# The mixers' own transfers and the residual's load issued by GpSimd's queue instead of SyncE's

## The chip, the cores and the metric

The kernel runs on one core of a Trainium2 chip. The metric is the device time of one execution in microseconds (us). The engines are named as in the profile: PE is TensorE (the matrix engine), DVE is VectorE, ACT is ScalarE, POOL is GpSimd and SP is SyncE, which here does nothing but issue transfers (DMAs). Each engine works through its own instructions in a fixed order; between engines there are only semaphores.

## The reference

One layer of a hybrid decoder over 256 tokens of width 2048, all in float32. Four mixers, each 512 wide, read parts of one projection, and their results go through a common output projection; then comes a SwiGLU of 5632 hidden columns and a final norm.

```python
n = rmsnorm(x, attn_norm[l])
u = n @ w_in[l]
u_gdn, u_mlstm, u_rglru, u_rwkv = jnp.split(u, MIXER_SPLITS, axis=-1)
y_gdn = gated_deltanet(u_gdn, ...)
y_mlstm = mlstm(u_mlstm, ...)
y_rglru = rglru_block(u_rglru, ...)
y_rwkv = rwkv7_time_mix(u_rwkv, ...)
mix = jnp.concatenate([y.astype(x.dtype) for y in (y_gdn, y_mlstm, y_rglru, y_rwkv)], axis=-1)
x = x + mix @ w_out[l]
n = rmsnorm(x, ffn_norm[l])
x = x + (jax.nn.silu(n @ ffn_w_gate[l]) * (n @ ffn_w_up[l])) @ ffn_w_down[l]
return rmsnorm(x, final_norm)
```

gated_deltanet and rwkv7_time_mix work in chunks of 64 tokens, and each needs the inverse of a triangular block per chunk and head. mlstm needs running sums and running maxima of its gates over the tokens.

## The kernel before

**Weights.** All weights lie in device memory as 404 units of 128x1024 float32 (512 KB). `raw()` loads a unit from SP's queue into one of four raw buffers; `halves()` makes two halves of it, whi on ACT (a copy rounded to the format that PE multiplies) and wlo on DVE (the rest), into four buffers each; `mm3()` multiplies with three matmuls (whi·hi, whi·lo, wlo·hi). In the profile the loads and the halves stand under L274, the matmuls under L169, L170 and L171, with the tiles big, mx and mxl as their results in PSUM.

**Mixers.** Each mixer is a Python generator: rw (rwkv7_time_mix, `rwkv_half`, one for each half of the heads), gd (gated_deltanet, `gdn_half`), ml (mlstm) and rg. While the big projections are written out, `tick` advances the generators, and their own small matmuls go through `Lag` (recorded as L409 and L413), so that the scheduler puts them between the big ones. The scheduler settles the order on every engine when the kernel is built.

**The transfers that the change touches**, all issued by SP before:

- rw: each half writes its triangular blocks to device memory (L622, eight pieces of 32x8x32) and loads them into the solver's tile (L625). `joint_solve` inverts all blocks together on DVE (L499, L500) and writes the inverse (L512) and, after a copy on DVE (L503), its transpose (L513) back to device memory, 64x1024 each. Each half loads its part of both into a tile XT (L660, L661: twelve transfers of 32x8x32 in all; sD_321 and sD_325 in the order's names). The first products that use them are the zu matmuls, `mx<-sD,sD 32x32`.
- gd: the same with L932, L933, L512, L513 (32x1024 here), L945 and L946 (fourteen transfers of 32x4x32). Its first products are copied by DVE in L955 and L963.
- ml: the gate weights (L782, L784), the running sums ncd (L822), the running maxima Md (L848), and for each half a broadcast of two rows of them over 128 partitions (`bcast_rows`, L866). L1059 and L1060 on DVE read Md's broadcast.
- `w_out`: four loads of the residual x, 512 KB each (L1196).

POOL before clears tiles, takes a few powers, issues one load for rg (L1419, 512 KB) and, late in the program, four broadcasts of the final norm's weights (L1301, 256 KB each). L763 on DVE is the mixers' convolution.

Of the kernel before, what the change touches and what calls it, by code (L numbers as in the profile page):

```python
# [12 lines left out]
P = 128  # L13
T = 256
# [491 lines left out]
def joint_solve(em, key, q0, nq, steps, free=False):  # L506
    nc = em.nc
    while not all((key + "A", h) in em.mix for h in range(2)):
        yield
    yield from solve_blocks(em, q0, nq, steps)  # L510
    dt, dtt = (em.dp.tile([nq, 32, 32], F32, name=em.nm("dr"), tag=em.nm("dr")) for _ in range(2))
    nc.sync.dma_start(dt, em.inv[q0 : q0 + nq])  # L512
    nc.sync.dma_start(dtt, em.blk[q0 : q0 + nq])  # L513
    em.mix[key + "S"] = (dt, dtt)
    if free:
        em.free(*em.solver)


def rwkv_half(em, hf, LX, R, K, V):
    nc = em.nc  # L520
# [12 lines left out]
    z = lora(em.lw[0:64], LX[0:64, 0:T])  # L533
# [3 lines left out]
    z = lora(em.lw[64:128], LX[64:128, 0:T])  # L537
    a = em.S()
# [4 lines left out]
    z = lora(em.g2, LX[:, T : 2 * T])  # L543
# [23 lines left out]
    z = yield from sums(em, em.bdr, sq, 1)  # L567
# [28 lines left out]
    z = yield from sums(em, em.bdr, t1, 1)  # L596
# [6 lines left out]
    for cc in range(2):  # L603
        zz = [em.mx(), em.mx()]
        g = em.S(2)
        gv = g.rearrange("p (c j h n) -> p c j h n", c=2, j=2, h=2)
        for h in range(2):
            rows = slice(64 * h, 64 * h + 64)
            for ci in range(2):
                for j in range(2):  # L610
                    u = j * 4 + 2 * cc + ci
                    ts = slice(u * 64, u * 64 + 64)
                    o = (ci * 2 + j) * P
                    em.pe.matmul(zz[h][:, o : o + P], KB[rows, u * P : u * P + P], ARv[rows, :, ts], start=True, stop=True)
        for h in range(2):
            nc.vector.tensor_tensor(g.rearrange("p (u h n) -> p u h n", h=2, n=P)[:, :, h, :], zz[h].rearrange("p (u n) -> p u n", n=P), em.gm.unsqueeze(1).to_broadcast([P, 4, P]), op=ALU.mult)
        GM.append(g)
        dr = em.dp.tile([32, 32, 32], F32, name=em.nm("dr"), tag=em.nm("dr")) if cc == 0 else dr
        for d in range(2):
            q0 = cc * 16 + d * 8  # L620
            src = g[64 + 32 * d : 96 + 32 * d, :].rearrange("p (u n) -> p u n", n=P)[:, :, 32 * d : 32 * d + 32]
            nc.sync.dma_start(dr[q0 : q0 + 8].rearrange("q s t -> s q t"), src)  # L622
        yield

    nc.sync.dma_start(blk3, dr)  # L625

    def gmv(c, h, s):
        return GM[c // 2][:, (c % 2) * 512 + h * P + s * 64 : (c % 2) * 512 + h * P + s * 64 + 64]
# [27 lines left out]
    for cc in range(2):  # L656
        for d in range(2):
            q0 = 32 * hf + cc * 16 + d * 8
            if d == 0:
                nc.sync.dma_start(XT.rearrange("p (u n) -> p u n", n=64)[64:96, cc * 8 : cc * 8 + 8, 32:64], dt[q0 : q0 + 8].rearrange("q s t -> s q t"))  # L660
            nc.sync.dma_start(XT.rearrange("p (u n) -> p u n", n=64)[64 + 32 * d : 96 + 32 * d, cc * 8 : cc * 8 + 8, 32 * d : 32 * d + 32], dtt[q0 : q0 + 8].rearrange("q s t -> s q t"))  # L661
    for _ in range(2):
        yield
    zu = em.mx()
# [113 lines left out]
def gates_load(em):  # L778
    nc, A = em.nc, em.A
    em.gw_ = em.S()  # L780
    em.gw = em.gw_[:, 0:256].rearrange("p (k n) -> p k n", k=KT)
    nc.sync.dma_start(em.gw_[:, 0:256], A["gate_w"])  # L782
    gp = em.const([16, 4], "gp")
    nc.sync.dma_start(gp[:, 0:2], A["gate_b"])  # L784
    nc.gpsimd.memset(gp[:, 2:3], -1.0)
    nc.gpsimd.memset(gp[0:8, 2:3], 1.0)
    em.gp = gp
    em.rs16 = em.gw_[0:16, 256:512]
    nc.gpsimd.memset(em.rs16, 1.0)
    nc.gpsimd.memset(em.rs16[0:8, 128:129], 0.0)  # L790


def gates_mm(em):
    nc = em.nc
    gs = em.S()
    ghi, glo = (gs.bitcast(F32R)[:, i * 256 : i * 256 + 256].rearrange("p (k n) -> p k n", k=KT) for i in range(2))
    nc.scalar.activation(ghi, em.gw, AF.Copy)
    nc.vector.tensor_tensor(glo, em.gw, ghi.bitcast(F32), op=ALU.subtract)
    z = em.mx()
    o = z[0:16, 0:T]  # L800
    for k in range(KT):
        em.mm3(o, ghi[:, k, :], glo[:, k, :], em.nhi[:, k, :], em.nlo[:, k, :], start=k == 0, stop=k == KT - 1)
    em.free(gs)
    g = em.S(2)
    gp = em.gp
    U, V = g[0:16, 0:T], g[0:16, T : 2 * T]
    N, B = g[0:16, 2 * T : 3 * T], g[0:16, 3 * T : 4 * T]
    nc.scalar.activation(U, o, AF.Identity, bias=gp[:, 0:1])
    nc.scalar.activation(gp[:, 1:2], gp[:, 1:2], AF.Exp)
    nc.scalar.activation(B, U, AF.Tanh, scale=0.5)  # L810
    nc.vector.tensor_scalar(B, B, 0.5, 0.5, op0=ALU.mult, op1=ALU.add)
    nc.scalar.activation(N, U, AF.Abs)
    nc.scalar.activation(N, N, AF.Exp, scale=-1.0)
    nc.vector.tensor_scalar(V, U, gp[:, 2:3], 0.0, op0=ALU.mult, op1=ALU.max)
    yield
    nc.scalar.activation(N, N, AF.Ln, bias=em.c_one[0:16])
    nc.vector.tensor_tensor(V, V, N, op=ALU.add)
    nc.vector.tensor_scalar(V, V, gp[:, 1:2], None, op0=ALU.mult)
    nc.vector.tensor_tensor_scan(N, em.rs16, V, 0.0, op0=ALU.mult, op1=ALU.add)
    em.free(em.gw_)  # L820
    em.ncd = em.dp.tile([4, T], F32, name="ncd", tag="ncd")
    nc.sync.dma_start(em.ncd, N[0:4, :])  # L822
    t = em.mx()
    for i, r in enumerate((U, N, B)):
        for a in range(2):
            em.pe.transpose(t[:, (i * 2 + a) * 16 : (i * 2 + a) * 16 + 16], r[:, a * P : a * P + P], em.ident[0:16, 0:16])
    GT = em.const([P, 3, 2, 16], "GT")
    nc.vector.tensor_copy(GT.rearrange("p i a n -> p (i a n)"), t[:, 0:96])
    em.free(g)
    em.ncs = GT[:, 1]  # L830
    em.nbeta = em.const([P, 2, 4], "nbeta")
    nc.vector.tensor_scalar(em.nbeta, GT[:, 2, :, 4:8], -1.0, None, op0=ALU.mult)
    em.beta = GT[:, 2, :, 4:8]
    em.neg = em.const([P, 4], "neg")
    nc.scalar.activation(em.neg, GT[:, 1, 1, 0:4], AF.Exp, scale=-1.0)
    nc.vector.tensor_scalar(em.neg, em.neg, -1.0, None, op0=ALU.mult)
    yield

    em.c = em.const([P, 2, 4], "ccol")
    nc.vector.tensor_tensor(em.c, GT[:, 0, :, 8:12], GT[:, 1, :, 12:16], op=ALU.add)  # L840
    t = em.mx()
    for a in range(2):
        em.pe.transpose(t[0:4, a * P : a * P + P], em.c[:, a, :], em.ident)
    M = em.S()
    nc.vector.tensor_copy(M[0:4, T : 2 * T], t[0:4, 0:T])
    nc.vector.tensor_tensor_scan(M[0:4, 0:T], M[0:4, T : 2 * T], M[0:4, T : 2 * T], 0.0, op0=ALU.max, op1=ALU.max)
    em.Md = em.dp.tile([4, T], F32, name="Md", tag="Md")
    nc.sync.dma_start(em.Md, M[0:4, 0:T])  # L848
    yield
    t = em.mx()  # L850
    for a in range(2):
        em.pe.transpose(t[:, a * 4 : a * 4 + 4], M[0:4, a * P : a * P + P], em.ident[0:4, 0:4])
    em.free(M)
    em.M = em.const([P, 2, 4], "Mcol")
    nc.vector.tensor_copy(em.M.rearrange("p a n -> p (a n)"), t[:, 0:8])
    em.enm = em.const([P, 2, 4], "enm")
    nc.vector.tensor_tensor(em.enm, GT[:, 1, :, 12:16], em.M, op=ALU.subtract)
    nc.vector.tensor_scalar(em.enm, em.enm, 80.0, None, op0=ALU.min)
    nc.scalar.activation(em.enm, em.enm, AF.Exp)
    em.mix["gates"] = 1  # L860


def bcast_rows(em, d, hf):

    z = em.S(c="B")
    em.nc.sync.dma_start(z, d[2 * hf : 2 * hf + 2].rearrange("h t -> (h t)").partition_broadcast(P))  # L866
    return z


def gdn_half(em, hf, Q, K, V, SZ):  # L870
# [58 lines left out]
    dr = em.dp.tile([16, 32, 32], F32, name=em.nm("dr"), tag=em.nm("dr"))  # L929
    for b in range(4):  # L930
        r = slice(32 * b, 32 * b + 32)
        nc.sync.dma_start(dr[4 * b : 4 * b + 4].rearrange("q s t -> s q t"), u4(MT)[r, :, r])  # L932
    nc.sync.dma_start(blk3, dr)  # L933
    yield
    em.mix["gdA", hf] = 0
    while "gdS" not in em.mix:
# [5 lines left out]
    for b in range(4):  # L942
        r = slice(32 * b, 32 * b + 32)
        if b != 3:
            nc.sync.dma_start(u4(X)[r, :, r], dt[16 * hf + 4 * b : 16 * hf + 4 * b + 4].rearrange("q s t -> s q t"))  # L945
        nc.sync.dma_start(u4(XT)[r, :, r], dtt[16 * hf + 4 * b : 16 * hf + 4 * b + 4].rearrange("q s t -> s q t"))  # L946
    for _ in range(4):
        yield
    UU = em.S(c="B")
# [239 lines left out]
def w_out(em):  # L1189
# [3 lines left out]
    for n in range(2):  # L1193
        for a in range(2):
            em.x[a, n] = em.S(2)
            nc.sync.dma_start(em.x[a, n], xin[:, a, n * 1024 : n * 1024 + 1024])  # L1196
    em.xq = {(a, q): em.x[a, q // 2][:, (q % 2) * 512 : (q % 2) * 512 + 512] for a in range(2) for q in range(4)}
    row = {"gd": 0, "ml": 4, "rg": 8, "rw": 12}
    sp = {}
# [278 lines left out]
```

## Time and profile before

| what | value |
| --- | --- |
| median of three runs | 1264.97 us (1264.12 to 1267.12) |
| the profiled execution's own time | 1266.58 us |
| its span, first to last instruction | 1264.9 us |
| mean granted clock of PE | 0.991 of full speed |
| busy: PE, DVE, ACT, POOL | 1240.5, 787.1, 639.4, 33.3 us |
| moved by transfers | 226.97 MB, mean 179 GB/s |
| a raw load, issue to landing (median of 404) | 3.8 us |

The span is the time from the first to the last instruction. A busy share says how long an engine worked, not whether it held others up: that is read from the waits. The granted clock is the share of PE's full speed that it was given. All rows below come from the same profiled execution.

### The profile page before, as it was taken

Reading aid. Unit: us, or ns where it says so; the run is one execution under the profiler, and the core shown is the slowest. Engines: PE = TensorE matmul, PEld = TensorE weight load, DVE = VectorE, ACT = ScalarE, POOL = GpSimd, SP = SyncE. Lnnn points to the kernel's source line nnn. Section 1 sums busy time; section 2 is a strip of 40 time slices with the busy share of each in tenths; the row PEclk is TensorE's granted clock in tenths of the full one; section 3 lists DMA queues with packets and bytes.
Section 4 is the critical chain, followed back from the end, with each engine's and each line's share of the span. In section 5 each row is a group of like instructions: output and inputs, shape, how many; then the busy total and the mean of one; then the engine's idle time right before and its main releaser. Section 6 shows DMA issues by size and latency. Waiting matters only on the chain.

```text
span 1264.9 us, 18346 instructions
## 1 busy us (share of the span) xinstructions
PE 1240.5 (98%) x7216; PEld 1070.8 (85%) x7216; DVE 787.1 (62%) x1095; ACT 639.4 (51%) x849; POOL 33.3 (3%) x65
## 2 busy tenths in 40 slices
PE   9999999999998999999999999999999999999997
PEld 8899999997998688888888888888888888888885
DVE  7876799666799776744454444444444455556554
ACT  7755785446644354644444444434444454455443
POOL 1100000000000010000000000000000000001000
PEclk9999999999999899999999999999999999999998
DMA  8555436353654536566666666666666666666663
GB/s 330 184 179 144 141 124 202 94 188 108 209 160 136 166 110 200 173 190 190 186 197 186 185 198 185 204 210 190 192 186 193 190 184 197 189 195 187 197 190 109
DMA packets 72198, 226.97 MB, mean 179 GB/s; under 512 B 15752, under 2 KB 16016, under 8 KB 72112
## 3 DMA queue, kind: packets, MB, share of 16 engines
q1 hardware_dynamic: 71504, 224.14, 57.9%
q0 software_dynamic: 464, 1.57, 0.4%
q8 instruction: 56, 0.92, 0.3%
q14 instruction: 30, 0.25, 0.1%
q10 hardware_dynamic: 144, 0.10, 0.0%
HBM read 222.49 MB, written 3.28 MB: 178 GB/s over the span
## 4 chain that ended last, share of the span: by engine, by line
PE 88%; DVE 6%; DMA 2%; issue 1%; ACT 1%; SPq 0%; POOL 0%; DVEq 0%; POOLq 0%; ACTq 0%
PE big L170 15%; PE big L171 15%; PE big L169 15%; PE mx L169 10%; PE mx L171 10%; PE mx L170 10%; PE mx L409 5%; DVE wlo L274 2%; PE big L277 2%; PE mxl L169 2%; PE mxl L171 2%; PE mxl L170 2%; DMA raw<-in_units 1%; DVE sD L500 1%; DVE sD L499 1%
## 5 line engine op out<-in xcount | busy, mean ns | idle before, releaser
L274 DVE TENSOR_TENSOR wlo<-raw,whi 128x1024 fp32r<-128x1024 f32 x396 | 485.3, 1227 | 365.6 <-ACT whi L274 363.3
L274 ACT ACTIVATE whi<-raw 128x1024 fp32r<-128x1024 f32 x396 | 418.2, 1057 | 441.3 <-PE big L171 308.4
L170 PE MATMUL big<-wlo,nhi 128*128 128x512 f32 (+1 forms) x464 | 161.6, 348 | 1.2 <-DVE wlo L274 1.2
L169 PE MATMUL big<-whi,nhi 128*128 128x512 f32 (+1 forms) x464 | 161.4, 348 | 0.4 <-ACT whi L274 0.4
L171 PE MATMUL big<-whi,nlo 128*128 128x512 f32 (+1 forms) x464 | 161.4, 348 | 0.0
L171 PE MATMUL big<-nhi,wlo 128*128 128x256 f32 x544 | 157.3, 290 | 3.1 <-DVE wlo L274 3.1
L170 PE MATMUL big<-nlo,whi 128*128 128x256 f32 x544 | 158.5, 291 | 0.0
L169 PE MATMUL big<-nhi,whi 128*128 128x256 f32 x544 | 157.4, 289 | 0.0
L169 PE MATMUL mx<-whi,nhi 128*128 128x512 f32 x352 | 138.2, 393 | 0.0
L171 PE MATMUL mx<-whi,nlo 128*128 128x512 f32 x352 | 137.3, 390 | 0.0
L170 PE MATMUL mx<-wlo,nhi 128*128 128x512 f32 x352 | 137.1, 390 | 0.0
L171 PEld LDWEIGHTS big<-nhi,wlo 128*128 128x128 f32 x544 | 105.3, 194 | 4.6 <-DVE wlo L274 3.3
L170 PEld LDWEIGHTS big<-nlo,whi 128*128 128x128 f32 x544 | 105.3, 194 | 2.1 <-issue 0.7
L169 PEld LDWEIGHTS big<-nhi,whi 128*128 128x128 f32 x544 | 105.3, 194 | 1.3 <-issue 0.3
L170 PEld LDWEIGHTS big<-wlo,nhi 128*128 128x128 f32 x464 | 88.5, 191 | 12.4 <-DVE wlo L274 1.6
L169 PEld LDWEIGHTS big<-whi,nhi 128*128 128x128 f32 x464 | 88.4, 191 | 11.5 <-ACT whi L274 0.8
L171 PEld LDWEIGHTS big<-whi,nlo 128*128 128x128 f32 x464 | 88.5, 191 | 10.9
L170 PE MATMUL big<-wlo,sA 128*128 128x512 f32 x220 | 86.5, 393 | 1.0 <-DVE wlo L274 1.0
L169 PE MATMUL big<-whi,sA 128*128 128x512 f32 x220 | 86.7, 394 | 0.0
L171 PE MATMUL big<-whi,sA 128*128 128x512 f32 x220 | 86.6, 393 | 0.0
L169 PE MATMUL mx<-whi,sA 128*128 128x512 f32 x208 | 81.4, 391 | 0.7 <-ACT sA L1181 0.7
L170 PE MATMUL mx<-wlo,sA 128*128 128x512 f32 x208 | 81.1, 390 | 0.0
(433 smaller groups left out, 1758.9 us busy)
## 6 DMA issues: line engine op xcount, KB each, us to landing
raw<-in_units SPq DMA_DIRECT2D x404, 512.0 KB, 3.8
sD<-in_x SPq DMA_DIRECT2D x8, 512.0 KB, 5.4
sD<-in_xT SPq DMA_DIRECT2D x4, 512.0 KB, 6.2
out_y<-sD SPq DMA_DIRECT2D x8, 256.0 KB, 2.9
sA<-in_final_norm POOLq DMA_DIRECT2D x4, 256.0 KB, 5.5
sD<-in_lora SPq DMA_DIRECT2D x1, 512.0 KB, 7.2
sD<-in_rglru POOLq DMA_DIRECT2D x1, 512.0 KB, 4.1
dr<-sD SPq DMA_DIRECT2D x2, 256.0 KB, 4.6
```

The costliest lines, as they stand in the source:

```text
L169: i = nc.tensor.matmul(out, ahi, bhi, start=start, stop=False, skip_group_check=True)
L170: nc.tensor.matmul(out, ahi, blo, start=False, stop=False, skip_group_check=True)
L171: self.last_mm = nc.tensor.matmul(out, alo, bhi, start=False, stop=stop, skip_group_check=True)
L274: i = fn(*a, **k)
L277: i = fn(*a, **k)
L409: return self.em.nc.tensor.matmul(*a, **k)
L499: nc.vector.tensor_tensor(tv, col, row, op=ALU.mult)
L500: nc.vector.tensor_tensor(inv[:, j + 1 : n, 0:b], inv[:, j + 1 : n, 0:b], tv, op=ALU.add)
```

## The change

The issuing engine of the transfers listed above becomes POOL (`nc.gpsimd` for `nc.sync`); their sizes, addresses and places in the program's text stay. SP keeps the loads of the weights, of x at the start, and the stores of the result. In SP's order 46 rows go, and POOL's order grows from 66 rows to 106 (a row can stand for several instructions of one kind).

```diff
 def joint_solve(em, key, q0, nq, steps, free=False):
...
-    nc.sync.dma_start(dt, em.inv[q0 : q0 + nq])
-    nc.sync.dma_start(dtt, em.blk[q0 : q0 + nq])
+    nc.gpsimd.dma_start(dt, em.inv[q0 : q0 + nq])
+    nc.gpsimd.dma_start(dtt, em.blk[q0 : q0 + nq])
...
 def rwkv_half(em, hf, LX, R, K, V):
...
-            nc.sync.dma_start(dr[q0 : q0 + 8].rearrange("q s t -> s q t"), src)
+            nc.gpsimd.dma_start(dr[q0 : q0 + 8].rearrange("q s t -> s q t"), src)
...
-    nc.sync.dma_start(blk3, dr)
+    nc.gpsimd.dma_start(blk3, dr)
...
             if d == 0:
-                nc.sync.dma_start(XT.rearrange("p (u n) -> p u n", n=64)[64:96, cc * 8 : cc * 8 + 8, 32:64], dt[q0 : q0 + 8].rearrange("q s t -> s q t"))
-            nc.sync.dma_start(XT.rearrange("p (u n) -> p u n", n=64)[64 + 32 * d : 96 + 32 * d, cc * 8 : cc * 8 + 8, 32 * d : 32 * d + 32], dtt[q0 : q0 + 8].rearrange("q s t -> s q t"))
+                nc.gpsimd.dma_start(XT.rearrange("p (u n) -> p u n", n=64)[64:96, cc * 8 : cc * 8 + 8, 32:64], dt[q0 : q0 + 8].rearrange("q s t -> s q t"))
+            nc.gpsimd.dma_start(XT.rearrange("p (u n) -> p u n", n=64)[64 + 32 * d : 96 + 32 * d, cc * 8 : cc * 8 + 8, 32 * d : 32 * d + 32], dtt[q0 : q0 + 8].rearrange("q s t -> s q t"))
...
 def gates_load(em):
...
-    nc.sync.dma_start(em.gw_[:, 0:256], A["gate_w"])
+    nc.gpsimd.dma_start(em.gw_[:, 0:256], A["gate_w"])
...
-    nc.sync.dma_start(gp[:, 0:2], A["gate_b"])
+    nc.gpsimd.dma_start(gp[:, 0:2], A["gate_b"])
...
 def gates_mm(em):
...
-    nc.sync.dma_start(em.ncd, N[0:4, :])
+    nc.gpsimd.dma_start(em.ncd, N[0:4, :])
...
-    nc.sync.dma_start(em.Md, M[0:4, 0:T])
+    nc.gpsimd.dma_start(em.Md, M[0:4, 0:T])
...
 def bcast_rows(em, d, hf):
...
-    em.nc.sync.dma_start(z, d[2 * hf : 2 * hf + 2].rearrange("h t -> (h t)").partition_broadcast(P))
+    em.nc.gpsimd.dma_start(z, d[2 * hf : 2 * hf + 2].rearrange("h t -> (h t)").partition_broadcast(P))
...
 def gdn_half(em, hf, Q, K, V, SZ):
...
-        nc.sync.dma_start(dr[4 * b : 4 * b + 4].rearrange("q s t -> s q t"), u4(MT)[r, :, r])
-    nc.sync.dma_start(blk3, dr)
+        nc.gpsimd.dma_start(dr[4 * b : 4 * b + 4].rearrange("q s t -> s q t"), u4(MT)[r, :, r])
+    nc.gpsimd.dma_start(blk3, dr)
...
-            nc.sync.dma_start(u4(X)[r, :, r], dt[16 * hf + 4 * b : 16 * hf + 4 * b + 4].rearrange("q s t -> s q t"))
-        nc.sync.dma_start(u4(XT)[r, :, r], dtt[16 * hf + 4 * b : 16 * hf + 4 * b + 4].rearrange("q s t -> s q t"))
+            nc.gpsimd.dma_start(u4(X)[r, :, r], dt[16 * hf + 4 * b : 16 * hf + 4 * b + 4].rearrange("q s t -> s q t"))
+        nc.gpsimd.dma_start(u4(XT)[r, :, r], dtt[16 * hf + 4 * b : 16 * hf + 4 * b + 4].rearrange("q s t -> s q t"))
...
 def w_out(em):
...
-            nc.sync.dma_start(em.x[a, n], xin[:, a, n * 1024 : n * 1024 + 1024])
+            nc.gpsimd.dma_start(em.x[a, n], xin[:, a, n * 1024 : n * 1024 + 1024])
```

The change also moves instructions on the engines, since the scheduler orders by when it takes things to be ready. POOL's new order, in the return of the rw solve (dr_2508 and dr_2509 are the inverse and its transpose in device memory):

```order
+L512 DMA dr_2508<-sD_83_778 64x1024
+L513 DMA dr_2509<-sD_82_777 64x1024
+L660 DMA sD_321_2512<-dr_2508 32x8x32 x2
+L661 DMA sD_321_2512<-dr_2509 32x8x32 x4
+L660 DMA sD_325_2550<-dr_2508 32x8x32
+L661 DMA sD_325_2550<-dr_2509 32x8x32 x2
+L660 DMA sD_325_2550<-dr_2508 32x8x32
+L661 DMA sD_325_2550<-dr_2509 32x8x32 x2
```

All transfers into sD_321 stand ahead of those into sD_325, as on SP before; here they stand in POOL's queue. On PE, at the first products of the rw solve (mx_2658 is zu of the tile sD_325, big_2771 a big projection):

```order
@@ -1443,4 +1443,5 @@
 L169 MATMUL big_2771<-whi_2774,nhi 128x256
 L170 MATMUL big_2771<-wlo_2775,nhi 128x256
+L409 MATMUL mx_2658<-sD_325_2550,sD_142_1143 32x32 x8
 L171 MATMUL big_2771<-whi_2774,nlo 128x256
 L169 MATMUL big_2771<-whi_2774,nhi 128x256
@@ -1461,6 +1462,6 @@
 L169 MATMUL big_2771<-whi_2846,nhi 128x256
 L170 MATMUL big_2771<-wlo_2847,nhi 128x256
-L409 MATMUL mx_2658<-sD_325_2550,sD_142_1143 32x32 x8
 L171 MATMUL big_2771<-whi_2846,nlo 128x256
+L409 MATMUL mx_2658<-sD_325_2550,sD_153_1219 32x32 x8
```

The first eight zu products moved 18 big matmuls earlier in PE's order. On DVE, where Md's last broadcast (sB_563) is read first, and in the gd return:

```order
 L763 SCALAR_TENSOR_TENSOR sA_539_4113<-big_3958,chan,sA_539_4113 128x254
+L1059 TENSOR_SCALAR sA_576_4416<-sB_563_4305,ccol 128x256
 L763 SCALAR_TENSOR_TENSOR sA_539_4113<-big_3958,chan,sA_539_4113 128x253
 L274 TENSOR_TENSOR wlo_4310<-raw_4307,whi_4309 128x1024
 L774 SCALAR_TENSOR_TENSOR sA_539_4113<-sA_561_4299,sA_539_4113 128x512
 L499 TENSOR_TENSOR sD_84_779<-sD_82_777,sD_83_778 32x31
-L1059 TENSOR_SCALAR sA_576_4416<-sB_563_4305,ccol 128x256
```

L1059 moved ahead of a convolution step, of wlo_4310, of L774 and of a step of the gd solver. In the gd return:

```order
+L274 TENSOR_TENSOR wlo_5174<-raw_5171,whi_5173 128x1024
 L774 SCALAR_TENSOR_TENSOR sA_636_4916<-sD_660_5015,sA_636_4916 128x512
 L955 COPY sB_655_4983<-mx_4984 32x128
-L274 TENSOR_TENSOR wlo_5174<-raw_5171,whi_5173 128x1024
+L274 TENSOR_TENSOR wlo_5192<-raw_5189,whi_5191 128x1024
 L955 COPY sB_655_4983<-mx_4984 32x128
 L963 COPY sA_618_4758<-mx_4995 32x4x32
```

Two wlo moved ahead of the two L955 copies of the first solve products of gd, one each.

## Rows read from the trace of the kernel before

**Rows 1.** the page's part 1, busy time, share of the span, instructions

```profile
PE 1240.5 (98%) x7216; PEld 1070.8 (85%) x7216; DVE 787.1 (62%) x1095; ACT 639.4 (51%) x849; POOL 33.3 (3%) x65
```

**Rows 2.** waits of SP's queue: waited for, us in total, times, longest us

```profile
SPq L274 <- DVE wlo L274: 916.4, 363, 15.2
```

**Rows 3.** waits of PE, the whole list has 12 rows

```profile
PE big L171 <- DVE wlo L274: 3.1, 1, 3.1
...
PE mx L413 <- ACT sA L1090: 1.7, 1, 1.7
...
PE mx L409 <- DVE sB L955: 1.2, 1, 1.2
```

**Rows 4.** timeline of SP's queue, 213 to 226 us: start, duration, instruction

```profile
214.37 0.45 SPq L513 DMA_DIRECT2D dr<-sD  x1
...
217.68 0.34 SPq L660 DMA_DIRECT2D sD<-dr  x1
219.46 0.82 SPq L661 DMA_DIRECT2D sD<-dr  x2
...
221.86 0.39 SPq L660 DMA_DIRECT2D sD<-dr  x1
...
224.82 1.34 SPq L274 DMA_DIRECT2D raw<-in_units  x3
```

**Rows 5.** DMA issues of 213 to 226 us: KB each, median us to landing

```profile
dr<-sD SPq DMA_DIRECT2D x2, 256.0 KB, 4.6
sD<-dr SPq DMA_DIRECT2D x12, 32.0 KB, 1.8
```

**Rows 6.** timeline of PE, 218 to 231 us

```profile
225.03 0.69 PE L409 MATMUL mx<-sD,sD 32*32 32x32 f32 x16
```

**Rows 7.** groups of POOL: busy us, mean ns of one, idle before

```profile
L1301 POOL DMA_DIRECT2D sA<-in_final_norm x4 | 2.2, 550 | 313.0 <-ACT whi L274 270.0 <-PE big L1279 43.0
...
L1419 POOL DMA_DIRECT2D sD<-in_rglru x1 | 0.8, 766 | 2.1 <-PE big L171 2.1
```

**Rows 8.** the page's part 6, issues by POOL: KB each, us to landing

```profile
sA<-in_final_norm POOLq DMA_DIRECT2D x4, 256.0 KB, 5.5
...
sD<-in_rglru POOLq DMA_DIRECT2D x1, 512.0 KB, 4.1
```

**Rows 9.** windows: us, PE, PEld, DVE, ACT, POOL busy, PEclk, DMA share, GB/s

```profile
8.00:36.00 28.00, 27.98 (x233) 27.90 (x233) 22.19 (x51) 21.00 (x38) 1.85 (x3) 1.00 0.93 354
62.00:70.00 8.00, 8.00 (x50) 8.00 (x49) 8.00 (x11) 1.72 (x3) 0.00 (x0) 0.68 0.81 261
380.00:410.00 30.00, 26.82 (x220) 26.19 (x220) 27.09 (x59) 13.27 (x28) 3.07 (x3) 1.00 0.45 133
425.00:430.00 5.00, 4.76 (x30) 3.31 (x23) 3.32 (x7) 1.86 (x3) 0.00 (x0) 0.55 0.91 318
430.00:435.00 5.00, 5.00 (x23) 3.62 (x22) 2.98 (x4) 1.65 (x2) 0.00 (x0) 0.77 0.47 136
```

**Rows 10.** chain of waits, 345 to 430 us: start, us, what

```profile
349.99 3.78 DMA sB<-Md
```

**Rows 11.** timeline of DVE, 349 to 356 us

```profile
352.02 1.51 DVE L763 SCALAR_TENSOR_TENSOR sA<-big,chan,sA 128x255 f32<-128x255 f32 x3
353.77 1.23 DVE L274 TENSOR_TENSOR wlo<-raw,whi 128x1024 fp32r<-128x1024 f32 x1 [0.24 <-DMA sB<-Md]
...
355.84 0.35 DVE L1059 TENSOR_SCALAR sA<-sB,ccol 128x256 f32<-128x256 f32 x1
```

**Rows 12.** timeline of SP's queue, 409 to 422 us

```profile
413.76 0.39 SPq L945 DMA_DIRECT2D sA<-dr  x1
...
420.64 1.32 SPq L274 DMA_DIRECT2D raw<-in_units  x3
```

**Rows 13.** timeline of DVE, 409 to 430 us

```profile
425.58 1.23 DVE L274 TENSOR_TENSOR wlo<-raw,whi 128x1024 fp32r<-128x1024 f32 x1 [1.06 <-ACT whi L274]
```

**Rows 14.** timeline of DVE, 210 to 216 us

```profile
213.24 1.10 DVE L503 COPY sD<-sD 64x1024 f32<-64x1024 f32 x1
```

## The prediction

> **What bounds the kernel now.** I read the busy times first: TensorE is busy for 98% of the span [rows 1], so a change gains only what TensorE waits for, and loses what it makes TensorE wait for. Then the list of TensorE's waits: twelve rows, some 15 us together, and each names a tile that VectorE or ScalarE writes; the longest is 3.1 us, and no row names a transfer [rows 3]. Then the waits of SP's own queue: 916 us in 363 waits are for VectorE to finish with an old raw buffer before the next unit may be loaded into it [rows 2]. SP is thus not short of time to issue; it stands idle most of the span, and the four raw buffers set when a load starts. Last I followed three places on the timelines: the return of the rw solve (213 to 230 us), the solve of gd (349 to 413 us) and its return (410 to 430 us). What counts there is when TensorE or VectorE first uses what a moved transfer brings.
>
> **What the change does, part by part.**
>
> *Taken off SP.* In the rw return SP is held from the issue at 217.68 until it issues raw loads again at 224.82 [rows 4], some 7 us. TensorE works through this without a gap into the first solve product at 225.03 [rows 6], on halves made earlier. With the block gone the loads come sooner, but nobody waited for them: 0 us. In the gd return the fourteen small issues run from 413.76 to the next raw load at 420.64 [rows 12]; that load is felt, since VectorE then waits 1.06 us for the whi made from it [rows 13]. By the order, VectorE's next L955 stands behind a wlo that it used to precede, so that the earlier load is partly paid back by a later copy. I put the two against each other and take 0 us; bounds: nothing, or the whole of the faster rival below.
>
> *The price of an issue on POOL.* No small strided transfer is issued by POOL in this trace. The nearest rows are L1301 with 550 ns and L1419 with 766 ns [rows 7]. A row of L660/L661 has 256 pieces of 128 bytes, against 128 rows of 2 or 4 KB there. If bytes decide, it costs the lower 0.55 us; if pieces decide, twice 0.6, or 1.2 us. I take 0.77 us, the dearer of the two rows that exist. SP's own rows for the same are 0.34 to 0.47 us each [rows 4].
>
> *The rw return.* L513 is issued at 214.37 once VectorE has made its copy [rows 4]; such a transfer takes 4.6 us at the median [rows 5], and SP could go on to L661 at 219.46 [rows 4]. On POOL I give it 0.3 us more (the row of L1419 lands at 4.1 for 512 KB [rows 8], a raw load of the same size on SP in 3.8, as the table of the profile says): 219.8. In POOL's new order four L661 for the first tile stand ahead of the first L660 of the other tile, sD_325, which the first solve product reads. Before, that L660 was issued at 221.86 [rows 4] and landed by 221.86 + 1.8 = 223.7 [rows 5], 1.4 us ahead of its use at 225.03. Now it begins at 219.8 + 4 × 0.77 = 222.9, and lands after 1.8 us [rows 5] plus the longer issue (0.77 less 0.4), at 225.0, say 225.3 with the 0.3 us above. TensorE comes for it earlier than before: the product has moved up by 18 big matmuls of 0.12 us, 2.2 us, to 222.8. The wait: **2.5 us**. With 0.55 us an issue it is 2.5 − 5 × 0.22 = 1.4, and 0.8 without the two 0.3 us; with 1.2 us it is 2.5 + 5 × 0.43 = 4.7. TensorE's order is fixed, so all work behind waits too.
>
> *TensorE's clock.* The longest wait, 3.1 us at 61 us [rows 3], was followed by a granted clock of 0.68 over 8 us [rows 9], so a part of it at 1.2 instead of 2.4 GHz: 0.32 × 8 = 2.6 us of work lost. The wait of 1.7 us on L1090 [rows 3], at 402 us, lies in a stretch granted 1.00 throughout [rows 9]. A wait of 2.5 us stands between the two; in proportion, (2.5 − 1.7) / (3.1 − 1.7) × 2.6 = **1.4 us**; bounds 0 and 2.6.
>
> *The last Md broadcast (L866).* Its slot comes free at 349.9, whichever queue issues it. On SP it was issued at 349.99 and took 3.78 us [rows 10]; VectorE was free 0.24 us before that and waited for it [rows 11]. From there to 413 us the chain of waits runs almost wholly through VectorE, which is busy for 27.1 of the 30 us from 380 on [rows 9], so that a delay here is kept. On POOL the same shape is there: L1301, a broadcast of 256 KB, lands in 5.5 us at the median [rows 8], 4.2 to 7.0 over its four. Those four went out in pairs; this one goes alone, and I take 5.0: landing at 354.9. In addition, VectorE's new order puts its first reader L1059 ahead of the third L763 of the trio that began at 352.02 [rows 11], so that it is reached near 352.9. VectorE waits 2.0 us, of which 0.24 was there before: **1.7 us**; bounds 0.6 (issue at once and 4.2) and 3.8 (7.0).
>
> *The rest.* gate_w and gate_b go out some 34 us earlier, into a stretch in which the DMA engines are busy at 0.93 with what TensorE starts on [rows 9]. 128 KB at that stretch's 354 GB/s is 0.37 us; little of it reaches TensorE: **0.1 us**, bounds 0 and 0.4. The rw solver's inputs (L622, L625), ncd, the gd return (the products need only the first of its tiles early, which holds up to 1.2 us an issue) and the residual loads, used from 428 us on, stay hidden; POOL itself has 33 us of work in the span [rows 1]. If that cover failed in the gd return, the price would be about 1 us at 1.2 us an issue.
>
> **Sum:** 0 + 2.5 + 1.4 + 1.7 + 0.1 = 5.7 us. The profiled execution took 1266.58 us (its span is 1264.9), so 1272.3; that execution lies 1.6 us above the median of 1264.97 us, so a median of **1270.7 us**. A measurement of this kernel can tell about 0.2%, 2.5 us, from no change.
>
> **A rule on transfers issued by GpSimd.** VectorE's copy L503 lies on POOL's issue of L512: 64x1024 in 1.10 us [rows 14], which is 1.07 ns for an element of a partition. The Trainium skill's page "SBUF — State Buffer", in its box on the "DVE blocks DMA" trap, says that GpSimd can't write descriptors while VectorE runs an fp32 copy from SBUF to SBUF in a mode that takes the shared port pair. By that rule POOL's L512 would not be out before 214.3, and L513, which follows it, would start about 0.7 us later. At that rate the row shows no doubled mode, so the trace speaks against the rule's case here, and I give it a small chance.
>
> **Rivals.**
> - *Nothing to be seen.* Issues at 0.55 us, landings as quick as on SP: 0.8 us in the rw return, no loss of clock, 0.6 us at L866: +1.4, or 1266.4 us. For it: no row of TensorE's waits named a transfer [rows 3]; against it: the two places have only 1.4 and 0 us of slack.
> - *Faster.* In the gd return raw loads start some 7 us earlier. TensorE's waits there (1.2 us on L955 [rows 3] and 0.24 on L963) and the clock behind them, 0.55 over 5 us and 0.77 over 5 us [rows 9], 0.45 × 5 + 0.23 × 5 = 3.4 us, go away: −4.9 us, or 1260.1 if nothing else is lost. It decides the sign once the rw return and L866 together cost under 2.4 us (4.9 less the 2.5 that can be told). With the quick prices above (1.4) it gives 1261.5 us. Against it: L955 now stands behind the wlo of the next unit.
> - *Much slower.* Pieces decide: 1.2 us an issue, 4.7 us of wait in the rw return, 2.6 us of clock, 3.0 us at L866 (a landing of 6.3) and 1 us in the gd return: +11.3, or 1276.3 us.
> - *L512 held behind VectorE's copy.* +0.7 us in the rw return, all of it wait, on top of the sum: 1271.4 us. This is the case of the rule above.
>
> **How the numbers follow.** Forecast 0.40, the held L512 0.06, much slower 0.14: slower by over 0.2% together 0.60. Nothing to be seen 0.26. Faster 0.14. The range leaves out the outer half of the faster case and of the much slower one: 1262.5 to 1276.0 us; the likeliest case by itself spans 1268 to 1274.
>
> **What would show it.** A wait of TensorE near 223 us on a POOL transfer into sD_325, 1 to 5 us long; a granted clock under 1.00 in the 8 us behind it; a wait of VectorE for Md's broadcast at L1059 near 353 us, 2 us instead of 0.24; POOL's issues of L661 about 0.8 us apart; the stretch 425 to 435 us as before. The prediction is wrong if POOL's small issues take 0.4 us or less, or if TensorE's waits at 424 us vanish with their clock.

## The result, and the profile after

The changed kernel takes 1273.12 us (median of four runs, 1271.75 to 1273.77), against 1265.51 us for the kernel before on the same chip: a ratio of 1.0056, with a 95% interval of 1.004 to 1.0072. It is slower by 7.6 us where 5.7 were forecast. The profiled execution has a span of 1271.6 us, 6.7 more than before.

The list of TensorE's waits has a new first row (waited for, us in total, times, longest us):

```profile
PE mx L409 <- DMA sD<-dr: 3.8, 1, 3.8
PE big L171 <- DVE wlo L274: 3.2, 1, 3.2
...
PE mx L413 <- ACT sA L1090: 2.2, 1, 2.2
PE mx L409 <- DVE sB L955: 1.5, 1, 1.5
```

It answers to [rows 3], where no row named a transfer. The place is the rw return. PE's timeline there, and POOL's (start, duration, instruction, idle time before):

```profile
227.40 0.81 PE L409 MATMUL mx<-sD,sD 32*32 32x32 f32 x12 [3.83 <-DMA sD<-dr]
```

```profile
213.84 1.27 POOL L512 DMA_DIRECT2D dr<-sD  x1 [15.80 <-DVE sD L500]
215.30 0.55 POOL L513 DMA_DIRECT2D dr<-sD  x1 [0.18 <-DVE sA L763]
219.55 1.23 POOL L660 DMA_DIRECT2D sD<-dr  x2 [3.71 <-DMA dr<-sD]
220.77 2.30 POOL L661 DMA_DIRECT2D sD<-dr  x4
223.06 0.58 POOL L660 DMA_DIRECT2D sD<-dr  x1
```

The first transfer into sD_325 is issued at 223.06, behind six others, and TensorE comes for it at 227.40 − 3.83 = 223.57. The issues follow each other at 0.58 us, where 0.77 was taken. The transfers of 219.4 to 226.5 us, by their issues (KB each, median us to landing), answer to [rows 5]:

```profile
raw<-in_units SPq DMA_DIRECT2D x2, 512.0 KB, 5.3
sD<-dr POOLq DMA_DIRECT2D x12, 32.0 KB, 4.5
```

They land after 4.5 us instead of 1.8. More bytes move beside them. The stretch in which SP issued the twelve before, and the one in which POOL issues them now (us, busy PE, PEld, DVE, ACT, POOL, then PEclk, DMA share, GB/s):

```profile
217.60:224.80 7.20, 7.20 (x62) 7.20 (x61) 5.97 (x9) 4.65 (x7) 0.00 (x0) 1.00 0.51 114
```

```profile
219.50:226.50 7.00, 4.08 (x35) 3.87 (x33) 4.50 (x7) 2.08 (x4) 6.67 (x12) 0.95 0.88 257
```

Against the kernel before, TensorE came 1.5 us sooner (225.03 to 223.57), the transfer was issued 1.2 us later (221.86 to 223.06) and took 2.5 us longer (1.8 to 4.3, its landing taken as the end of the wait); less the slack of 1.4 us that it had, this is the wait of 3.8 us. Windows of four microseconds show what follows it:

```profile
220.00:224.00 4.00, 3.58 (x30) 3.37 (x29) 3.22 (x5) 1.67 (x3) 4.00 (x8) 1.00 0.89 263
224.00:228.00 4.00, 0.60 (x12) 0.63 (x13) 0.81 (x2) 0.00 (x0) 2.51 (x5) 0.73 0.90 246
228.00:232.00 4.00, 4.00 (x26) 3.94 (x24) 1.29 (x2) 1.42 (x2) 0.00 (x0) 0.50 0.06 12
232.00:236.00 4.00, 4.00 (x64) 3.60 (x63) 1.51 (x3) 1.06 (x1) 0.00 (x0) 0.92 0.46 135
```

TensorE runs at 0.50, that is at 1.2 GHz, from 228 to 232, and at 0.92 in the four behind: 0.50 × 4 + 0.08 × 4 = 2.3 us lost, besides the 3.8. That makes 6.1 of the 7.6 us; the other 1.5 have no row of their own. On VectorE's timeline the other forecast wait is there too, for Md's broadcast:

```profile
362.30 0.35 DVE L1059 TENSOR_SCALAR sA<-sB,ccol 128x256 f32<-128x256 f32 x1 [1.86 <-DMA sB<-Md]
```

It answers to the 0.24 us of [rows 11].

### The profile page after: what moved, and what is told of

Same layout as the page of the kernel before. It is cut to its first block, busy times and chain, and to the rows that moved or that the text cites. A ratio compares the mean times of both kernels' runs of the same rounds, so it can differ in the third digit from the quotient of the medians.

```text
span 1271.6 us, 18383 instructions
## 1 busy us (share of the span) xinstructions
PE 1241.5 (98%) x7216; PEld 1072.0 (84%) x7216; DVE 787.0 (62%) x1095; ACT 639.4 (50%) x849; POOL 68.2 (5%) x127
## 4 chain that ended last, share of the span: by engine, by line
PE 84%; DVE 8%; issue 3%; DMA 2%; ACT 2%; POOL 1%; DVEq 0%; POOLq 0%; SPq 0%; ACTq 0%
PE big L170 14%; PE big L171 14%; PE big L169 14%; PE mx L169 10%; PE mx L170 10%; PE mx L171 10%; PE mx L409 4%; DVE wlo L274 3%; PE big L277 2%; PE mxl L171 1%; PE mxl L170 1%; PE mxl L169 1%; DVE sD L500 1%; DVE sD L499 1%; DVE sA L763 1%
## 5 line engine op out<-in xcount | busy, mean ns | idle before, releaser
L169 PE MATMUL mx<-whi,sA 128*128 128x512 f32 x208 | 81.3, 391 | 0.7 <-ACT sA L1181 0.7
L171 PE MATMUL mx<-whi,sA 128*128 128x512 f32 x208 | 80.9, 389 | 0.0
```

The source lines that it names most:

```text
L169: i = nc.tensor.matmul(out, ahi, bhi, start=start, stop=False, skip_group_check=True)
L171: self.last_mm = nc.tensor.matmul(out, alo, bhi, start=False, stop=stop, skip_group_check=True)
```

## The experiments

Each was timed beside the kernel before; a ratio is to that kernel, with its 95% interval. They were timed in three series, so that ratios compare better than medians. One thousandth of the time is 1.3 us.

**The rw return back on SP** (a1_xt_sp):

```diff
-            nc.gpsimd.dma_start(XT..., dt or dtt ...)   # L660, L661
+            nc.sync.dma_start(XT..., dt or dtt ...)
```

> The changed kernel with only the twelve L660/L661 transfers of the rw return back on SP. Theory: the 3.8 us wait of TensorE at 227 us and the clock lost behind it (about 2.6 us) are the main loss, so both go and the time is 1273.1 - 6.4 = about 1266.7 us. Rival (the loss is spread over the moved transfers, or the wait reappears elsewhere): 1270 to 1273 us.

Measured: 1266.31 us, ratio 1.0001 (0.9992 to 1.001), as the theory had it. No row of TensorE's waits names a transfer any more. With these twelve back on SP no loss is left that can be told. A small loss elsewhere may still be balanced by the small gain that c1_rest shows below.

**The same twelve issued by ScalarE** (a2_xt_act):

```diff
-            nc.gpsimd.dma_start(XT..., dt or dtt ...)
+            nc.scalar.dma_start(XT..., dt or dtt ...)
```

> The changed kernel with the twelve L660/L661 transfers issued by ScalarE's queue. Theory A (sharing): they land in 4.3 to 4.6 us instead of 1.8 because the raw loads, no longer held back behind them on one queue, share the DMA engines; then they land late from ScalarE too (3.5 to 4.6 us) and TensorE waits 1.5 to 3 us, 1269 to 1272 us. Theory B (POOL's own queue makes pieces of 128 bytes land late): from ScalarE they land in about 1.8 us, TensorE waits under 0.5 us, 1266 to 1268 us.

Measured: 1272.34 us, ratio 1.0048 (1.0029 to 1.0068). Here the early and the late ones of the twelve can be told apart. The issues of 215 to 219 us, with a raw load among them, and those of 220.5 to 223 us, when SP issued none:

```profile
DMA packets 977, 1.10 MB, mean 276 GB/s; under 512 B 728, under 2 KB 728, under 8 KB 977
...
raw<-in_units SPq DMA_DIRECT2D x1, 512.0 KB, 4.8
sD<-dr ACTq DMA_DIRECT2D x7, 32.0 KB, 4.0
```

```profile
sD<-dr ACTq DMA_DIRECT2D x4, 32.0 KB, 2.0
```

From one queue, and not POOL's, they land in 4.0 us beside a raw load and in 2.0 us without one: this speaks for the sharing and against theory B. (The twelfth was issued between the two stretches.) The wait of TensorE for them was a little shorter than theory A had it, and the time a little longer:

```profile
221.94 0.66 PE L409 MATMUL mx<-sD,sD 32*32 32x32 f32 x16 [1.33 <-DMA sD<-dr]
```

Behind it the granted clock was 0.95 from 220 to 224 us and 0.63 from 224 to 228, another 1.7 us. The profiled execution, at 1267.51 us, is the fastest of the six, so that it can't account for the median. ScalarE's own work stood still beside its issues and their waits, which may be the rest and isn't shown:

```profile
222.69 0.48 ACT L759 ACTIVATE sA<-big,chan 128x256 f32<-128x256 f32 x1 [9.07 <-DMA sD<-dr]
```

**Short raw loads around the rw return** (b1_short); of seven units only a quarter of the columns is loaded and used four times, so their products are not the layer's:

```diff
+        n = 256 if self.short else UNIT
-        self.ch("sp", self.nc.sync.dma_start, raw, self.A["units"][UNIT_AT[key]])
+        self.ch("sp", self.nc.sync.dma_start, raw[:, 0:n], self.A["units"][UNIT_AT[key]][:, 0:n])
...
+        if self.short:
+            rv = raw[:, 0:n].unsqueeze(1).to_broadcast([P, nk, n])
```

> The changed kernel in which seven raw loads (those issued between about 205 and 230 us) bring only 256 of their 1024 columns, and the halves read these four times: those seven units are computed on the wrong weights; the order of all instructions stays. Theory A (sharing with the raw loads makes the small transfers late): L660/L661 land in 2 to 2.5 us instead of 4.4, TensorE's wait in the rw return falls from 3.8 to under 1 us, time 1266 to 1268 us. Theory B (POOL's queue itself): they still land in about 4 us, the wait stays above 2.5 us, 1270 to 1273 us.

Measured: 1267.64 us, ratio 1.0011 (1.0 to 1.0022). The issues of 217 to 225 us, the wait of TensorE (L415 is L409 here, since six lines were added above it), and a window:

```profile
sD<-dr POOLq DMA_DIRECT2D x12, 32.0 KB, 2.3
raw<-in_units SPq DMA_DIRECT2D x3, 128.0 KB, 2.4
```

```profile
PE mx L415 <- DMA sD<-dr: 0.9, 1, 0.9
```

```profile
220.00:224.00 4.00, 3.15 (x38) 2.93 (x37) 2.89 (x5) 1.42 (x2) 4.00 (x8) 1.00 0.50 117
```

Same queue, same order, same issues of 0.58 us: with fewer bytes beside them (117 GB/s, after 263) the twelve land in 2.3 us, and the wait falls from 3.8 to 0.9. The clock stays at 1.00 behind it, up to 240 us. This is theory A, in the landing, the wait and the time.

**Only the twelve moved** (b2_xt_only), the kernel before with L660 and L661 on POOL:

```diff
-            nc.sync.dma_start(XT..., dt or dtt ...)
+            nc.gpsimd.dma_start(XT..., dt or dtt ...)
```

> The kernel before with only the twelve L660/L661 on POOL. L512 is then not held by VectorE's copy and lands earlier (217.7 us), so the first transfer into sD_325 is issued at about 221.8 us and lands 4.4 us later at 226.2; TensorE comes at about 223.9 us (its first product has moved up by fewer matmuls than in the changed kernel). Theory: wait 2.3 us and 1 to 2.5 us of clock, 1269 to 1270.5 us, less than the whole change but clearly slower than before. Rival (the loss needs the other moves too): 1266 us.

Measured: 1275.09 us, ratio 1.0069 (1.005 to 1.0087): the loss is there without the other moves, and larger than expected. The issues of 216 to 224 us and the wait:

```profile
raw<-in_units SPq DMA_DIRECT2D x3, 512.0 KB, 6.4
sD<-dr POOLq DMA_DIRECT2D x12, 32.0 KB, 5.1
```

```profile
PE mx L409 <- DMA sD<-dr: 3.5, 1, 3.5
```

The twelve were issued some 3 us earlier than in the changed kernel, into a time in which three raw loads were issued as well, and took longer still, 5.1 us at the median. The first one into sD_325 was issued at 220.17 us, not at 221.8, and TensorE's wait for it ended at 226.38: 6.2 us, where the expectation had kept 4.4. The two errors cancel. The wait is longer than expected since TensorE came sooner, at 222.9 us instead of 223.9. By its ratio this kernel loses 1.6 us more than the whole change, which lies within the two intervals.

**VectorE's copy made by ScalarE** (a4_copy_act), for the time that POOL takes over L512:

```diff
-    nc.vector.tensor_copy(blk.rearrange("q s t -> q t s"), inv)
+    nc.scalar.activation(blk.rearrange("q s t -> q t s"), inv, AF.Copy)
```

> The changed kernel with the copy of L503 made by ScalarE instead of VectorE. If VectorE's copy holds POOL back while it issues L512, the two L512 issues take about 0.55 us instead of 1.27 and 0.97. If a transfer of 256 KB simply takes POOL longer, they stay at 1.0 to 1.3 us. The scheduler also puts one L660 of sD_325 ahead of the L661 here and TensorE's first products 3 us earlier, so the wait of TensorE may be anywhere from 1 to 4 us: the time, 1269 to 1273 us, tells little by itself.

Measured: 1271.77 us, ratio 1.005 (1.0032 to 1.0068). The line of L512 (duration in ns: least, median, most), after and here:

```profile
L512 POOL DMA_DIRECT2D dr<-sD x2: 967/1120/1272, 213.8 to 418.8; - x2
```

```profile
L512 POOL DMA_DIRECT2D dr<-sD x2: 552/566/580, 212.4 to 416.0; - x2
```

So it is VectorE's copy that holds POOL; the same copy by ScalarE, from 212.17 to 214.30 us, doesn't hold the issue of 0.58 us that lies inside it. In the changed kernel VectorE's copy stands beside the issue of 213.84 to 215.11:

```profile
213.89 1.12 DVE L503 COPY sD<-sD 64x1024 f32<-64x1024 f32 x1
```

It ends at 215.01, and POOL is done 0.1 us later. In the gd solve the copy ends at 419.63 and POOL at 419.74. The Trainium skill's page "SBUF — State Buffer", in its box on the "DVE blocks DMA" trap, has this rule; the trace agrees with it in what happens to the issue. In which mode the copy ran no row shows. TensorE's wait in the rw return was still 3.3 us in this kernel, so that the hold alone doesn't make the loss.

**The broadcasts back on SP** (b3_bcast_sp):

```diff
-    em.nc.gpsimd.dma_start(z, d[2 * hf : 2 * hf + 2]...)
+    em.nc.sync.dma_start(z, d[2 * hf : 2 * hf + 2]...)
```

> The changed kernel with only the four broadcasts L866 back on SP. VectorE's wait at L1059 (1.9 us) should shrink to what SP's broadcast of before gives (3.8 us to land, about 0.3 to 1 us of wait at the new place of L1059), and if the chain through VectorE keeps it, the time falls by about 1 us, to 1272 us; if that wait is made up before the gd return, 1273 us.

Measured: 1272.21 us, ratio 1.0048 (1.0034 to 1.0061). VectorE's wait at L1059 falls from 1.9 to 0.9 us, and the loss by 1 us, from a ratio of 1.0056 to 1.0048; the two intervals overlap, so that the size isn't shown.

**Only the gd return moved** (a3_gd_only), the kernel before with L945 and L946 on POOL:

```diff
-            nc.sync.dma_start(u4(X)[r, :, r], ...)
-        nc.sync.dma_start(u4(XT)[r, :, r], ...)
+            nc.gpsimd.dma_start(u4(X)[r, :, r], ...)
+        nc.gpsimd.dma_start(u4(XT)[r, :, r], ...)
```

> The kernel before with only the fourteen L945/L946 transfers of the gd return on POOL. Theory: in the changed kernel this place gives back about 2 us (raw loads 7 us earlier, shorter stretch of low clock), so here alone 1265.5 - 2 to 3.5 = 1262 to 1263.5 us. Rival (what was given back there was only delay already taken elsewhere, since VectorE was late): 1265 to 1266 us, no difference.

Measured: 1265.44 us, ratio 0.9996 (0.9987 to 1.0005): the rival's number. In this kernel SP issues raw loads from 414.5 us on, where before none went out between 413.76 and 420.64 [rows 12]. Earlier raw loads there are worth nothing that can be told by themselves.

**The rest alone** (c1_rest, and again as c1_again): on POOL stay the gate weights, L622, L625, ncd, Md's own write, L932, L933, L945, L946 and the residual; L660, L661, L866, L512 and L513 go back to SP.

> The changed kernel with what was found or suspected to cost put back on SP: L660/L661, L866, and L512/L513; gate weights, solver inputs, ncd, Md, the gd return and the residual's loads stay on POOL. Theory: no loss is left and the relief of SP is worth nothing by itself, 1265 to 1266.5 us, no difference from the kernel before. Rival (a gain was hidden under the losses): 1261 to 1263.5 us.

> The same kernel as c1_rest, beside the other one on the same chip. Theory (its gain of 0.14% is real): 0.9975 to 0.9995 of the kernel before. Rival: 0.9995 to 1.0005.

Measured: 1264.38 us, ratio 0.9986 (0.9974 to 0.9998), and 1265.12 us, ratio 0.9988 (0.9976 to 0.9999). Both intervals leave out 1, by 0.0002 and 0.0001, so that a gain of about 0.13% is likely; it is below the 0.2% that was called a difference ahead, and no run shows which of the moves left on POOL gives it. From a1_xt_sp to this kernel, with L866, L512 and L513 back on SP too, the ratio falls from 1.0001 to 0.9986: these three may cost some 2 us together, but the two intervals overlap.

**And with L932 and L933 back on SP** (c2_md_order):

```diff
-        nc.gpsimd.dma_start(dr[4 * b : 4 * b + 4]...)
-    nc.gpsimd.dma_start(blk3, dr)
+        nc.sync.dma_start(dr[4 * b : 4 * b + 4]...)
+    nc.sync.dma_start(blk3, dr)
```

> The last kernel with the gd solver's inputs (L932, L933) back on SP as well, so that VectorE's order has L1059 behind wlo and L774 again, as in the kernel before. Theory: the 1.5 us wait at L1059 is gone and the chain through VectorE from 354 to 404 us is about 1 us shorter, so about 1 us less than the last kernel: 1263.4 us, against 1266.4 of the kernel before a gain of 0.2%. Rival (its small gain was only the clock's chance of that series): 1265.5 to 1266.5 us, no difference from before.

Measured: 1265.19 us, ratio 0.9984 (0.9975 to 0.9993). VectorE's wait for Md's broadcast, in c1_again and here:

```profile
DVE sA L1059 <- DMA sB<-Md: 0.8, 1, 0.8
```

```profile
DVE wlo L274 <- DMA sB<-Md: 0.2, 1, 0.2
```

L1059 no longer waits, as expected, and wlo waits for 0.2 us as in the kernel before; but beside it on the same chip c1_again has 1265.12 us, and the microsecond expected is not there. By their ratios c1_again lies 1.5 us and this kernel 2 us below the kernel before.

## Why the prediction was right, point by point

The direction, the place and the range held; 7.6 us came where 5.7 were forecast. That the sum came so near is in part luck: it has too little for the rw return and its clock (3.9, where 6.1 are read) and 1.7 us for L866, of which no run shows more than about 1. Two of its numbers don't follow from their own terms, both small: the clock's proportion gives 1.5 us, not 1.4, and a landing of 4.2 gives a lower bound of 1.0 us for L866, not 0.6.

- *The rw return, 2.5 us.* It measured 3.8. The start was right: the transfer was forecast to be issued at 222.9 and was at 223.06, though from errors against each other: an issue of 0.58 us instead of 0.77, and a later start of L661, at 220.77 instead of 219.8, since the two L660 ahead of it had to wait for L512, which began 0.9 us later than on SP and was held by VectorE's copy. TensorE came at 223.57, 0.8 us later than forecast. With the landing of 2.2 us that the forecast used it would have waited 1.7 us. The step that failed is "lands after 1.8 us plus the longer issue". It took a landing measured on SP, in a stretch that SP itself, from 217.68 to 224.82, had kept free of new raw loads [rows 4], for a property of the transfer. Off SP, the raw loads run beside it, and the landing is 4.5 us; with those loads cut to a quarter it is 2.3 us from the same queue (b1_short), and from ScalarE's queue 4.0 us with a raw load and 2.0 without (a2_xt_act). What the earlier place of the product in TensorE's order adds was forecast, and no run separates it.
- *Taken off SP, 0 us.* "The loads come sooner, but nobody waited for them" is right for the loads, and misses what else they do: they share the DMA engines with the twelve. The relief was not worth nothing here: it made most of the loss, since without most of their bytes only 0.9 us of wait and a ratio of 1.0011 are left (b1_short).
- *The clock, 1.4 us.* 2.3 us are read in the profile after, within the bounds of 0 and 2.6, after a wait that was longer too. The scale by the length of the wait isn't borne out: 1.3 us in a2_xt_act were followed by 1.7 us of lost clock, and 2.2 us on L1090 in the changed kernel, at 411 us, by none (1.00 from 404 to 420 us).
- *L866, 1.7 us.* VectorE's wait grew from 0.24 to 1.86 us, so by 1.6: forecast and row agree. How much of it reaches the end isn't settled: about 1 us by b3_bcast_sp, within the noise. That 0.8 us less of wait for the same broadcast, from SP in both kernels, gained nothing (c2_md_order against c1_again) speaks against all of it being kept.
- *The start, 0.1 us, and the gd return, 0.* Neither shows in a run: a1_xt_sp, with all of these moved, equals the kernel before, and a3_gd_only too. c1_rest, which keeps them, is even a little faster.
- *The rivals.* L512 held behind VectorE's copy, given 0.06, is what happened to the issue, with 0.7 us (1.27 less 0.57): the argument against it, from the copy's rate [rows 14], was wrong. That these 0.7 us lengthened TensorE's wait isn't shown: with L512 on SP (b2_xt_only) it was 3.5 us. The faster rival was right that the raw loads start earlier in the gd return, and wrong in the price: not 4.9 us, but within 0.1% of nothing by itself, and a gain of 0.12% to 0.16% with the other harmless moves. The much slower one's price of 1.2 us an issue is refuted by 0.58.

## What to carry to other kernels

A queue that issues in order does more than issue: here SP's kept the large loads behind it out of the DMA engines while its short transfers ran. A short transfer taken off such a queue must be costed with those loads beside it, not with its old landing. Before short transfers that an engine waits for are moved, ask what the old queue will issue in their place; move those with slack (here the residual and the gate weights) and leave those without. A series of small issues in one queue might well begin with the one that is used first: six others stood ahead of it here, 3.5 us. No run tries that alone.

## What the runs showed of the hardware

TensorE's wait of about 3 us for wlo near 61 us is followed by a different clock from execution to execution. It lasts 3.1 us before, 3.2 after and 2.9 in a4_copy_act, and ends at 61.2, 61.4 and 61.4 us; the clock from 62 to 70 us is 0.68 before [rows 9], 0.79 after and 1.00 in a4_copy_act:

```profile
62.00:70.00 8.00, 8.00 (x56) 8.00 (x56) 8.00 (x11) 3.12 (x5) 0.00 (x0) 0.79 0.80 257
```

```profile
62.00:70.00 8.00, 8.00 (x69) 8.00 (x68) 8.00 (x11) 3.61 (x6) 0.00 (x0) 1.00 0.73 244
```

From 112 to 120 us, where TensorE waits for nothing and works on small products, the profile after has a clock of 0.79:

```profile
112.00:120.00 8.00, 8.00 (x34) 5.75 (x33) 4.16 (x7) 3.94 (x8) 0.00 (x0) 0.79 0.34 111
```

In the kernel a2_xt_act the same window has 1.00. The largest of these, 0.68 over 8 us, is worth 2.6 us, so two single profiles can't be subtracted to less than that; the ratios of many runs can. The other thing, given only 0.06 ahead, is a POOL issue that lasts as long as VectorE's copy beside it.
